# A hybrid attention, recurrence and latent-attention layer: sums of squares moved to VectorE, projection weights asked for earlier, and compression accumulators in other PSUM banks

## The chip, the cores and the metric

The kernel runs on one core of one Trainium2 chip. The metric is the device time of one execution in microseconds (us), given as the median of several runs. Five engines work side by side: TensorE (PE, with its weight loads as PEld), VectorE (DVE), ScalarE (ACT), GpSimd (POOL) and SyncE (SP, which only issues transfers here). Each takes its instructions in its own order and waits on semaphores for the others.

## The reference

One layer over 512 frames of 1024 channels (cut to what matters here):

```
h = rmsnorm(x, g_mix);  P = h @ w_in           # 7072 columns, split into parts
A: q, k, v 512 each     -> chunked banded softmax attention, 8 heads
B: q, f, i, g 512 each  -> HGRN2 gated recurrence, 8 heads
C: c_q 256, c_kv 128, k_rope 32 -> latent attention:
     q  = rmsnorm(c_q)  @ w_uq;  kv = rmsnorm(c_kv) @ w_ukv;  rotary on the rope parts
G: 3 x 1024 gate logits
x += (sum_n sigmoid(G_n) * (y_n @ w_branch[n])) @ w_out
x += relu(rmsnorm(x) @ w_ff1)^2 @ w_ff2;   out = rmsnorm(x)
```

All inputs and the output are float32.

## The kernel before

Activations are held transposed: channels on the 128 partitions, the 512 frames along the free dimension. Each float32 operand of a large product is split into a rounded high part and a low part (hi = the value cast to fp32r, lo = value - hi), and a product is three TensorE instructions, hi*hi, hi*lo and lo*hi (`mm3` at L225 to L228; `mm3_u` at L320 to L325 is the same with a stop after each). The mixing norm's gain is folded into x (`xgh`, `xgl`), and its row factor `rstd` is applied to the results afterwards, so that products can start before the norm is known.

**The order of work.** TensorE's instructions are issued in exactly the order of the program text. On all other engines and queues a planner lists the instructions ahead of time by its own estimate of when each is ready, with program order as priority; on the chip each engine then follows its list in order. Buffers of a tag (`bufs=3` and so on) are handed out by the planner as they come free, and whoever writes a reused buffer waits for its last reader.

**The opening stage (L340 to L430).** For each of the 8 channel blocks k, SP loads a block of x (`xt`) and half a block of the compression weights (`wc`, into one of two buffers `wr`). ScalarE makes `xgh` (L402), VectorE makes `xgl` (L403), `split` (L211 to L213) makes `wh` by ScalarE and `wl` by VectorE, and TensorE adds 12 products into four PSUM accumulators `pc` (c_q in two, c_kv, and the rotary key with its swapped copy). Two blocks k share one buffer `wh` and one `wl`; each of these tags has 3 buffers. ScalarE squares x (L419), and GpSimd adds the squares into `ss` (L421). At k = 2 the rotary angles are computed (`rotary`). The accumulators `pc0` to `pc2` take all three banks of the tag `acc`, `pc3` the one bank of `up`; the tags `sc` and `tp` have two banks each. After the loop the four accumulators are copied out to `c` (L427, L429).

**The queue of projections.** `project` (L432) and `project_nat` (L447) append units to a queue: 8 for the q and k of A (`aqk`, 24 products each, accumulated in an `acc` bank named `pj`), 2 for its v (`avn`), later those of B and the gates. `fill(n)` puts the next n products of the queue into TensorE's order wherever the text says so; the numbers stand in `TUNE`. Weights come through three steps: `load` asks for a 512 KB block on the POOL queue into a buffer of tag `wr` or `wh`, at most 2 ahead; `convert` lets ScalarE write its negated rounded copy into `wl` (L279), and a second, accumulating transfer of the same block on the POOL queue (L280) adds the weights to it, which leaves the low part. `get` takes the oldest converted block. `taken[0] % 5` chooses the tag:

```
tag, bufs = (("wr", 2), ("wh", 3))[taken[0] % 5 > 1]
```

**The norms (L480 to L510).** The squares of the three compressed blocks are made, `fill(s0 = 6)` puts in 6 products, and then three products with a matrix of ones sum over the channels: `pkv` (c_kv), `pst` (`ss`, the norm of x) and `pq` (c_q). VectorE and ScalarE turn these into `rk`, `rstd` and `rq` and scale the compressed blocks, and `fill(s1 = 30)` follows in TensorE's order.

**After that.** `csplit` splits the compressed blocks (`cnh`, `cnl`), `cweights` (L622) loads and splits small weight blocks, its low part by GpSimd, four products `pv` make C's v (banks `up`, `tp`, `sc`, `tp`), four steps prepare the first pair of heads, and the attention of C runs over 8 heads x 4 blocks of queries (`attention`, L568) with `fill` between its steps (`ca`, `cb`, `cd`). Up to the tail of that loop the fills take 281 of the 288 products in the queue; the rest goes into the tail. B's and the gates' units are appended only after it.

Of the kernel before, what the change touches and what calls it, by code (L numbers as in the profile page):

```python
# [32 lines left out]
PACE = 12  # L33

TUNE = dict(
    s0=6, s1=30, c0=3, c1=9, c2=18, ca=[5, 3, 3, 1, 3, 3, 3, 5], cb=[1, 0, 3, 5, 3, 1, 4, 4], cd=6, a0=9,
    aa=[7, 0, 6, 4], ab=[4, 2, 7, 5], ad=0, h0=60, ha=[7, 6, 5, 4, 5, 6, 2, 9, 3, 8, 5],
    hb=[8, 8, 5, 7, 6, 6, 5, 2, 20, 5, 4], n0=9,
)
# [101 lines left out]
def _body(ctx, tc, ap, dbgo):  # L141
# [8 lines left out]
    def f(t):  # L150
        return t.bitcast(F32)
# [12 lines left out]
    def acc(n="acc"):  # L164
        return ps.tile([P, S], F32, tag="acc", name=n, bufs=3)

    def pup(n="up"):
        return ps.tile([P, S], F32, tag="up", name=n, bufs=1)
# [4 lines left out]
    def ptp(n="tp"):  # L173
        return ps.tile([P, S], F32, tag="tp", name=n)
# [36 lines left out]
    def split(hi, lo, src):  # L211
        A.copy(hi, src)
        V.tensor_tensor(lo, src, f(hi), ALU.subtract)  # L213
# [11 lines left out]
    def mm3(out, wh, wl, xh, xl, start, stop, **kw):  # L225
        T.matmul(out, wh, xh, start=start, stop=False, **kw)  # L226
        T.matmul(out, wh, xl, start=False, stop=False, **kw)  # L227
        T.matmul(out, wl, xh, start=False, stop=stop, **kw)  # L228
# [34 lines left out]
    def load():  # L263

        while loads and len(raw) < 2:
            src = loads.pop(0)
            tag, bufs = (("wr", 2), ("wh", 3))[taken[0] % 5 > 1]
            taken[0] += 1
            hi = ws.tile([P, 1024], F32R, tag=tag, name="wh", bufs=bufs)
            G.dma_start(hi, src)  # L270
            raw.append((hi, src))
# [63 lines left out]
    with ExitStack() as st_ctx:  # L335
# [6 lines left out]
            T.matmul(warm[:, :P], ones, ones, start=True, stop=True)  # L342

        xt, wc = [], []
        pc = [acc(f"pc{i}") for i in range(3)] + [pup("pc3")]
        for k in range(NK):
            t = st.tile([P, S], F32, tag="xt", name="xt", bufs=8)
            nc.sync.dma_start(t, ap['xT'][k * P:(k + 1) * P, :])
# [12 lines left out]
        def rotary():  # L361

            def ct(n):
                return st.tile([P, 64], F32, tag="rp", name=n, bufs=6)
            pi = st.tile([P, 64], I32, name="rpi")
            G.dma_start(pi, bass.AP(tensor=ap['pos'].tensor, offset=0, ap=[[0, 16], [64, 8], [1, 64]]))
            ang = ct("ang")
            V.tensor_copy(ang, pi)
            V.tensor_scalar(ang, ang, freq, None, ALU.mult)
            n_ = ct("n_")  # L370
            V.tensor_scalar(n_, ang, 1.0 / (2 * np.pi), 12582912.0, ALU.mult, ALU.add)
            V.tensor_scalar(n_, n_, -12582912.0, None, ALU.add)
            rest = 2 * np.pi
            for i in range(5):
                part = float(np.float32(rest))
                if i < 4:
                    e = int(np.floor(np.log2(rest))) - 7
                    part = float(np.floor(rest / 2.0 ** e) * 2.0 ** e)
                rest -= part
                V.scalar_tensor_tensor(ang, n_, -part, ang, ALU.mult, ALU.add)  # L380
            V.tensor_scalar(ang, ang, -3.1415925, 3.1415925, ALU.max, ALU.min)
            sn = ct("sn")
            A.activation(sn, ang, AF.Sin)
            V.scalar_tensor_tensor(ang, ang, -1.0, ang, ALU.mult, ALU.max)
            cs = ct("cs")
            last_sin = A.activation(cs, ang, AF.Sin, bias=halfpi, scale=-1.0)
            tables("natural_log_exp_and_others", last_sin)
            return (("dcos", cs, cosT, 0, 4), ("dsin", sn, sinT, 2, 6))
# [5 lines left out]
                for i in range(first, first + n):  # L394
                    nc.sync.dma_start(dst[16 * i:16 * i + 16, :], d)

        make_identity(nc, ident)
        ss = st.tile([P, S], F32, name="ss")
        for k in range(NK):
            xh = act.tile([P, S], F32R, tag="act", name="xgh")  # L400
            xl = act.tile([P, S], F32R, tag="act", name="xgl")
            A.activation(xh, xt[k], AF.Copy, scale=g_mix[:, k:k + 1])  # L402
            V.scalar_tensor_tensor(xl, xt[k], g_mix[:, k:k + 1], f(xh), ALU.mult, ALU.subtract)  # L403
            xg.append((xh, xl))
            j = k % 2
            if j == 0:
                wh = ws.tile([P, 1024], F32R, tag="wh", name="wh")
                wl = ws.tile([P, 1024], F32R, tag="wl", name="wl")
            c = slice(j * 448, (j + 1) * 448)
            split(wh[:, c], wl[:, c], wc[k][:, c])  # L410
            for i in range(4):
                m = P if i < 3 else 64
                c = slice(j * 448 + i * P, j * 448 + i * P + m)
                mm3(pc[i][:m], wh[:, c], wl[:, c], xh, xl, k == 0, k == NK - 1)
            if k == 2:
                rotation = rotary()
            for j in (() if k == 0 else (k - 1,) if k < NK - 1 else (k - 1, k)):
                sq = ss if j == 0 else st.tile([P, S], F32, tag="sq", name="sq", bufs=2)
                A.activation(sq, xt[j], AF.Square)  # L419
                if j:  # L420
                    G.tensor_tensor(ss, ss, sq, ALU.add)  # L421
        crw = []
        for i in range(4):
            t = fqt(f"c{i}")
            m = P if i < 3 else 64
            if i % 2:
                V.tensor_copy(t[:m], pc[i][:m])  # L427
            else:
                A.copy(t[:m], pc[i][:m])  # L429
            crw.append(t)  # L430

        def project(src, n, name, out, then=None):  # L432
            def run():
                i = len(out)
                pz = acc("pj")
                yield from gemm_u(pz, get(), xg, NK)
                t = fqt(name)
                V.tensor_tensor(t, pz, rstd, ALU.mult)
                out.append(t)
                if then:  # L440
                    then(i, t)
                yield 1
            for i in range(n):
                last = add([src[i]], run)
            return last

        def project_nat(src, name, pool, out, halves=(0, 1)):  # L447

# [21 lines left out]
                last = add([src[half, kk] for kk in range(2)], half_run(half))  # L470
            return last

        aqk, avn, bz, bvn, bq, cums, late = [], [], [], [], [], [], {}
        project(ap['w_aqk'], 8, "aqk", aqk)
        a_done = project_nat(ap['w_av'], "avn", nap, avn)
        convert()
        convert()
        spread(rotation)

# [115 lines left out]
    with ExitStack() as at_ctx:  # L595
# [8 lines left out]
        with ExitStack() as c_ctx:  # L604
# [14 lines left out]
            ckv = [csplit(crw[2])]  # L619
            cqn = [csplit(t) for t in crw[:2]]  # L620

            def cweights(src, n):  # L622
                r = cp.tile([P, 640], F32, tag="cwr", name="cwr", bufs=1)
                nc.sync.dma_start(r[:, :n], src)
                hi = cp.tile([P, 640], F32R, tag="cwh", name="cwh", bufs=1)
                lo = cp.tile([P, 640], F32R, tag="cwl", name="cwl", bufs=1)
                A.copy(hi[:, :n], r[:, :n])
                G.tensor_tensor(lo[:, :n], r[:, :n], f(hi[:, :n]), ALU.subtract)
                return hi, lo


            wvh, wvl = cweights(ap['w_uv'], 512)
            v2 = []
            for s in range(NST):
                pv = (pup, ptp, psc, ptp)[s]("pv")
# [772 lines left out]
```

## Time and profile before

| | us |
|---|---|
| median of 3 runs | 954.14 |
| lowest and highest | 952.27 to 956.85 |
| the profiled execution's own time | 951.3 |
| its span in the trace | 949.5 |
| mean granted TensorE clock | 0.984 of full speed |

| engine | busy us | share of the span |
|---|---|---|
| PE | 907.1 | 96% |
| DVE | 657.1 | 69% |
| ACT | 557.5 | 59% |
| POOL | 201.4 | 21% |

The profiled execution's time is the span and 1.8 us around it. Times in the views are counted from the start of the span. The opening stage and the norms lie in its first 51 us, and the attention of C ends at about 164 us. A matmul's duration in a row is longer than its share of TensorE, since consecutive ones overlap; what counts is the distance from one start to the next.

### The profile page before, as it was taken

Reading aid. Unit: us, or ns where it says so; the run is one execution under the profiler, and the core shown is the slowest. Engines: PE = TensorE matmul, PEld = TensorE weight load, DVE = VectorE, ACT = ScalarE, POOL = GpSimd, SP = SyncE. Lnnn points to the kernel's source line nnn. Section 1 sums busy time; section 2 is a strip of 40 time slices with the busy share of each in tenths; the row PEclk is TensorE's granted clock in tenths of the full one; section 3 lists DMA queues with packets and bytes.
Section 4 is the critical chain, followed back from the end, with each engine's and each line's share of the span. In section 5 each row is a group of like instructions: output and inputs, shape, how many; then the busy total and the mean of one; then the engine's idle time right before and its main releaser. Section 6 shows DMA issues by size and latency. Waiting matters only on the chain.

```text
span 949.5 us, 13636 instructions
## 1 busy us (share of the span) xinstructions
PE 907.1 (96%) x5070; PEld 784.4 (83%) x5070; DVE 657.1 (69%) x1212; ACT 557.5 (59%) x983; POOL 201.4 (21%) x264
## 2 busy tenths in 40 slices
PE   8889999998998899999999999999999999999993
PEld 6578898987877788888888888889989988998992
DVE  6488888787878869788472454455456745885686
ACT  7556778787776656757552444555365346435663
POOL 4422101111154424333122122001101100110002
PEclk9899999999999999999999999999999999999996
DMA  6865445666666475758689784238835862893522
GB/s 200 212 132 120 91 93 115 140 123 125 139 128 144 97 157 111 155 115 195 137 203 207 165 236 140 89 92 196 227 108 133 209 190 89 182 240 111 132 47 89
DMA packets 42947, 138.08 MB, mean 145 GB/s; under 512 B 5056, under 2 KB 9296, under 8 KB 42880
## 3 DMA queue, kind: packets, MB, share of 16 engines
q0 software_dynamic: 23104, 83.95, 43.8%
q1 hardware_dynamic: 19776, 53.26, 16.8%
q8 instruction: 40, 0.66, 0.3%
q14 instruction: 27, 0.22, 0.1%
HBM read 135.03 MB, written 2.16 MB: 144 GB/s over the span
## 4 chain that ended last, share of the span: by engine, by line
PE 72%; DVE 15%; issue 4%; DMA 4%; ACT 3%; POOL 1%; SPq 0%; DVEq 0%; POOLq 0%; ACTq 0%
PE p L227 6%; PE p L228 6%; PE p L226 6%; PE pj L325 3%; PE pj L321 3%; PE pj L323 3%; PE pg L321 3%; PE pg L325 3%; PE pg L323 3%; PE sa L228 2%; PE sa L227 2%; PE sa L226 2%; PE sc L522 2%; DMA bias<-in_rel 2%; PE po L227 2%
## 5 line engine op out<-in xcount | busy, mean ns | idle before, releaser
L221 ACT CAST wh<-wr 128x1024 fp32r<-128x1024 f32 x64 | 67.2, 1050 | 111.0 <-PE p L227 24.8
L222 DVE TENSOR_TENSOR wl<-wr,wh 128x1024 fp32r<-128x1024 f32 x64 | 78.3, 1223 | 75.9 <-ACT wh L221 67.5
L226 PE MATMUL p<-x2h,wh 128*128 128x512 f32 x256 | 100.0, 391 | 0.0
L227 PE MATMUL p<-x2l,wh 128*128 128x512 f32 x256 | 99.6, 389 | 0.0
L228 PE MATMUL p<-x2h,wl 128*128 128x512 f32 x256 | 99.6, 389 | 0.0
L279 ACT ACTIVATE wl<-wh 128x1024 fp32r<-128x1024 f32 x64 | 67.7, 1057 | 48.4 <-PE pg L325 26.9
L321 PE MATMUL pg<-xgh,wh 128*128 128x512 f32 x192 | 76.7, 400 | 0.0
L325 PE MATMUL pg<-xgh,wl 128*128 128x512 f32 x192 | 76.6, 399 | 0.0
L323 PE MATMUL pg<-xgl,wh 128*128 128x512 f32 x192 | 76.3, 398 | 0.0
L321 PE MATMUL pj<-xgh,wh 128*128 128x512 f32 x160 | 65.0, 406 | 2.4 <-ACT c L429 2.4
L323 PE MATMUL pj<-xgl,wh 128*128 128x512 f32 x160 | 65.7, 410 | 0.0
L325 PE MATMUL pj<-xgh,wl 128*128 128x512 f32 x160 | 64.3, 402 | 0.8 <-DMA wl<-in_w_aqk 0.8
L1256 POOL DMA_DIRECT2D cw<-in_w_ff x16 | 13.7, 858 | 219.2 <-DVE wl L1236 216.4
L226 PEld LDWEIGHTS p<-x2h,wh 128*128 128x128 f32 x256 | 48.1, 188 | 10.1 <-issue 0.2
L227 PEld LDWEIGHTS p<-x2l,wh 128*128 128x128 f32 x256 | 48.1, 188 | 10.1 <-issue 0.2
L228 PEld LDWEIGHTS p<-x2h,wl 128*128 128x128 f32 x256 | 48.1, 188 | 10.0
L227 PE MATMUL sa<-rl,wh 128*128 128x256 f32 x192 | 54.3, 283 | 0.0
L228 PE MATMUL sa<-rh,wl 128*128 128x256 f32 x192 | 54.3, 283 | 0.0
L226 PE MATMUL sa<-rh,wh 128*128 128x256 f32 x192 | 54.3, 283 | 0.0
L1236 DVE TENSOR_TENSOR wl<-cw,wh 128x1024 fp32r<-128x1024 f32 x24 | 29.3, 1223 | 29.9 <-ACT wh L1235 29.9
L1235 ACT CAST wh<-cw 128x1024 fp32r<-128x1024 f32 x24 | 25.2, 1050 | 35.0 <-PE sc L227 11.1
L321 PEld LDWEIGHTS pg<-xgh,wh 128*128 128x128 f32 x192 | 36.9, 192 | 7.8 <-DVE tg L884 0.4
(406 smaller groups left out, 2807.7 us busy)
## 6 DMA issues: line engine op xcount, KB each, us to landing
wr<-in_w_ff SPq DMA_DIRECT2D x56, 512.0 KB, 3.5
wh<-in_w_g POOLq DMA_DIRECT2D x24, 512.0 KB, 3.9
wl<-in_w_g POOLq DMA_DIRECT2D x24, 512.0 KB, 6.1
cw<-in_w_ff POOLq DMA_DIRECT2D x24, 512.0 KB, 5.6
wh<-in_w_br POOLq DMA_DIRECT2D x12, 512.0 KB, 3.8
wl<-in_w_br POOLq DMA_DIRECT2D x12, 512.0 KB, 6.1
wh<-in_w_aqk POOLq DMA_DIRECT2D x8, 512.0 KB, 4.4
wl<-in_w_aqk POOLq DMA_DIRECT2D x8, 512.0 KB, 6.4
```

The costliest lines, as they stand in the source:

```text
L221: A.copy(hi[:, :n], r[:, :n])
L222: (eng or G).tensor_tensor(lo[:, :n], r[:, :n], f(hi[:, :n]), ALU.subtract)
L226: T.matmul(out, wh, xh, start=start, stop=False, **kw)
L227: T.matmul(out, wh, xl, start=False, stop=False, **kw)
L228: T.matmul(out, wl, xh, start=False, stop=stop, **kw)
L279: A.activation(lo, f(hi), AF.Copy, scale=-1.0)
L321: T.matmul(out, wh, xh, start=start, stop=False, **kw)
L323: T.matmul(out, wh, xl, start=False, stop=False, **kw)
L325: T.matmul(out, wl, xh, start=False, stop=stop, **kw)
L522: T.matmul(sc[:, :n], l[:, t * P:(t + 1) * P], r[:, :n], start=i == 0, stop=i == len(scores) - 1)
L1235: A.copy(hi, r)
L1236: V.tensor_tensor(lo, r, f(hi), ALU.subtract)
```

## The change

- **Squares:** the additions into `ss` go from GpSimd to VectorE (7 of them). The squares are made one step later (blocks 0 and 1 at k = 2).
- **First step:** at k = 0 the weights are split before `xgh` and `xgl` are made; at the other k the order stays.
- **Weights of the projections:** `aqk` is put into the queue inside the loop, after the products of k = 4, with a `load()` there, and the first `convert()` comes at k = 6. One `convert()` is left behind the loop.
- **Buffers of the loads:** the first three of every five go into `wh`, the other two into `wr` (before: the first two into `wr`).
- **Banks:** `pc0` in `acc`, `pc1` and `pc2` in `tp`, `pc3` in `up` as before.
- **`s1`:** 36 products behind the norms' sums, before 30.
- **`cweights` for C's v:** its low part is made by VectorE.

```diff
-    s0=6, s1=30, c0=3, c1=9, c2=18, ...
+    s0=6, s1=36, c0=3, c1=9, c2=18, ...
...
-            tag, bufs = (("wr", 2), ("wh", 3))[taken[0] % 5 > 1]
+            tag, bufs = (("wr", 2), ("wh", 3))[taken[0] % 5 < 3]
...
-        pc = [acc(f"pc{i}") for i in range(3)] + [pup("pc3")]
+        pc = [acc("pc0"), ptp("pc1"), ptp("pc2"), pup("pc3")]
...
         for k in range(NK):
...
+            if k == 0:
+                split(wh[:, c], wl[:, c], wc[k][:, c])
             A.activation(xh, xt[k], AF.Copy, scale=g_mix[:, k:k + 1])
             V.scalar_tensor_tensor(xl, xt[k], g_mix[:, k:k + 1], f(xh), ALU.mult, ALU.subtract)
             xg.append((xh, xl))
...
-            split(wh[:, c], wl[:, c], wc[k][:, c])
+            if k:
+                split(wh[:, c], wl[:, c], wc[k][:, c])
             for i in range(4):
...
             if k == 2:
                 rotation = rotary()
-            for j in (() if k == 0 else (k - 1,) if k < NK - 1 else (k - 1, k)):
+            if k == 4:
+                project(ap['w_aqk'], 8, "aqk", aqk)
+                load()
+            if k == 6:
+                convert()
+            for j in (() if k < 2 else (k - 2, k - 1) if k == 2 else (k - 1,) if k < NK - 1 else (k - 1, k)):
                 sq = ss if j == 0 else st.tile([P, S], F32, tag="sq", name="sq", bufs=2)
                 A.activation(sq, xt[j], AF.Square)
                 if j:
-                    G.tensor_tensor(ss, ss, sq, ALU.add)
+                    V.tensor_tensor(ss, ss, sq, ALU.add)
...
-        project(ap['w_aqk'], 8, "aqk", aqk)
         a_done = project_nat(ap['w_av'], "avn", nap, avn)
         convert()
-        convert()
...
-            def cweights(src, n):
+            def cweights(src, n, eng=None):
...
-                G.tensor_tensor(lo[:, :n], r[:, :n], f(hi[:, :n]), ALU.subtract)
+                (eng or G).tensor_tensor(lo[:, :n], r[:, :n], f(hi[:, :n]), ALU.subtract)
...
-            wvh, wvl = cweights(ap['w_uv'], 512)
+            wvh, wvl = cweights(ap['w_uv'], 512, V)
```

`project` itself moves up in the text unchanged, so that the loop can call it.

## Rows read from the trace of the kernel before

**Rows 1.** Busy time by stretch: us, length, PE PEld DVE ACT POOL, PEclk, DMA, GB/s.

```profile
7.19:29.95 22.76, 22.58 (x96) 16.58 (x96) 18.47 (x27) 16.13 (x27) 13.40 (x15) 1.00 0.72 214
29.95:39.88 9.93, 6.73 (x13) 3.43 (x13) 2.40 (x4) 4.64 (x7) 3.68 (x5) 0.66 1.04 239
39.88:50.70 10.82, 8.15 (x35) 5.91 (x33) 8.45 (x15) 6.67 (x11) 1.43 (x2) 1.00 0.61 135
50.70:157.50 106.80, 106.56 (x624) 92.95 (x624) 93.66 (x240) 76.86 (x169) 20.78 (x24) 1.00 0.53 111
157.50:164.50 7.00, 5.47 (x41) 4.67 (x40) 4.84 (x10) 6.07 (x13) 1.11 (x2) 1.00 0.44 105
```

**Rows 2.** TensorE's waits, first 60 us: us in total, times, longest.

```profile
PE pj L321 <- ACT c L429: 2.4, 1, 2.4
...
PE pv L228 <- DVE cnl L213: 1.6, 1, 1.6
...
PE pv L226 <- ACT cnh L212: 1.1, 1, 1.1
PE pj L325 <- DMA wl<-in_w_aqk: 0.8, 1, 0.8
```

**Rows 3.** Timeline of TensorE, 24 to 60 us: start, us, instruction, idle before it.

```profile
24.05 0.39 PE L228 MATMUL pc<-xgh,wl 128*64 128x512 f32 x1
...
29.56 0.39 PE L228 MATMUL pc<-xgh,wl 128*64 128x512 f32 x1
32.30 0.66 PE L321 MATMUL pj<-xgh,wh 128*128 128x512 f32 x1 [2.36 <-ACT c L429]
...
36.12 1.91 PE L492 MATMUL pkv<-csq,ones 128*128 128x512 f32 x2
37.82 1.76 PE L493 MATMUL pst<-ss,ones 128*128 128x512 f32 x2
...
50.70 0.50 PE L228 MATMUL pv<-cwh,cnl 128*128 128x512 f32 x1 [1.61 <-DVE cnl L213]
```

**Rows 4.** Timeline of VectorE, 24 to 60 us.

```profile
34.47 0.86 DVE L489 TENSOR_TENSOR csq<-csq 128x512 f32<-128x512 f32 x1 [3.25 <-ACT csq L488]
39.62 0.69 DVE L498 TENSOR_SCALAR vx<-pst 128x512 f32<-128x512 f32 x1 [4.28 <-PE pst L493]
```

**Rows 5.** Timeline of ScalarE, 24 to 60 us.

```profile
30.72 1.06 ACT L279 ACTIVATE wl<-wh 128x1024 fp32r<-128x1024 f32 x1 [3.10 <-DVE c L427]
31.68 1.06 ACT L429 COPY c<-pc 128x512 f32<-128x512 f32 x2
...
47.68 0.62 ACT L212 CAST cnh<-c 128x512 fp32r<-128x512 f32 x1
```

**Rows 6.** Timeline of GpSimd, 20 to 60 us.

```profile
28.54 0.94 POOL L280 DMA_DIRECT2D wl<-in_w_aqk  x1
```

**Rows 7.** Timeline of TensorE, 290 to 300 us.

```profile
297.05 0.36 PE L226 MATMUL sl<-qbh,kxh 128*128 128x256 f32 x1 [2.65 <-ACT d L988]
```

**Rows 8.** Timeline of all engines, first 20 us.

```profile
6.59 0.55 ACT L212 CAST wh<-wr 128x448 fp32r<-128x448 f32 x1
...
7.19 0.50 PE L226 MATMUL pc<-xgh,wh 128*128 128x512 f32 x1 [1.24 <-ACT wh L212]
...
7.42 0.62 DVE L213 TENSOR_TENSOR wl<-wr,wh 128x448 fp32r<-128x448 f32 x1
...
8.10 0.50 PE L228 MATMUL pc<-xgh,wl 128*128 128x512 f32 x1 [0.17 <-DVE wl L213]
```

**Rows 9.** Groups of instructions, first 30 us: busy, mean ns, idle before.

```profile
L421 POOL TENSOR_TENSOR ss<-ss,sq 128x512 f32<-128x512 f32 x7 | 10.2, 1453 | 11.8 <-DMA dcos<-cs 6.1 <-ACT sq L419 5.5
...
L403 DVE SCALAR_TENSOR_TENSOR xgl<-xt,cst,xgh 128x512 fp32r<-128x512 f32 x8 | 7.8, 980 | 2.2 <-ACT xgh L402 2.2
L213 DVE TENSOR_TENSOR wl<-wr,wh 128x448 fp32r<-128x448 f32 x8 | 7.3, 912 | 0.0
```

**Rows 10.** DMA issues of the first 60 us: KB each, median us to landing.

```profile
wl<-in_w_aqk POOLq DMA_DIRECT2D x5, 512.0 KB, 6.8
```

More of the change, by code (lines that the diff above doesn't have):

```diff
@@ L35 @@
 TUNE = dict(
-    s0=6, s1=30, c0=3, c1=9, c2=18, ca=[5, 3, 3, 1, 3, 3, 3, 5], cb=[1, 0, 3, 5, 3, 1, 4, 4], cd=6, a0=9,
+    s0=6, s1=36, c0=3, c1=9, c2=18, ca=[5, 3, 3, 1, 3, 3, 3, 5], cb=[1, 0, 3, 5, 3, 1, 4, 4], cd=6, a0=9,
     aa=[7, 0, 6, 4], ab=[4, 2, 7, 5], ad=0, h0=60, ha=[7, 6, 5, 4, 5, 6, 2, 9, 3, 8, 5],
@@ L395, in spread @@
                     nc.sync.dma_start(dst[16 * i:16 * i + 16, :], d)
[L397 to L409, printed above, removed]
-            split(wh[:, c], wl[:, c], wc[k][:, c])
[L411 to L416, printed above, removed]
-            for j in (() if k == 0 else (k - 1,) if k < NK - 1 else (k - 1, k)):
-                sq = ss if j == 0 else st.tile([P, S], F32, tag="sq", name="sq", bufs=2)
-                A.activation(sq, xt[j], AF.Square)
-                if j:
-                    G.tensor_tensor(ss, ss, sq, ALU.add)
[L422 to L430, printed above, removed]
         def project(src, n, name, out, then=None):
@@ L445, in project @@
             return last
+        make_identity(nc, ident)
+        aqk, avn, bz, bvn, bq, cums, late = [], [], [], [], [], [], {}
+        ss = st.tile([P, S], F32, name="ss")
+        for k in range(NK):
+            xh = act.tile([P, S], F32R, tag="act", name="xgh")
+            xl = act.tile([P, S], F32R, tag="act", name="xgl")
+            j = k % 2
+            if j == 0:
+                wh = ws.tile([P, 1024], F32R, tag="wh", name="wh")
+                wl = ws.tile([P, 1024], F32R, tag="wl", name="wl")
+            c = slice(j * 448, (j + 1) * 448)
+            if k == 0:
+                split(wh[:, c], wl[:, c], wc[k][:, c])
+            A.activation(xh, xt[k], AF.Copy, scale=g_mix[:, k:k + 1])
+            V.scalar_tensor_tensor(xl, xt[k], g_mix[:, k:k + 1], f(xh), ALU.mult, ALU.subtract)
+            xg.append((xh, xl))
+            if k:
+                split(wh[:, c], wl[:, c], wc[k][:, c])
+            for i in range(4):
+                m = P if i < 3 else 64
+                c = slice(j * 448 + i * P, j * 448 + i * P + m)
+                mm3(pc[i][:m], wh[:, c], wl[:, c], xh, xl, k == 0, k == NK - 1)
+            if k == 2:
+                rotation = rotary()
+            if k == 4:
[4 more added lines that the diff above has]
+            for j in (() if k < 2 else (k - 2, k - 1) if k == 2 else (k - 1,) if k < NK - 1 else (k - 1, k)):
+                sq = ss if j == 0 else st.tile([P, S], F32, tag="sq", name="sq", bufs=2)
+                A.activation(sq, xt[j], AF.Square)
+                if j:
+                    V.tensor_tensor(ss, ss, sq, ALU.add)
+        crw = []
+        for i in range(4):
+            t = fqt(f"c{i}")
+            m = P if i < 3 else 64
+            if i % 2:
+                V.tensor_copy(t[:m], pc[i][:m])
+            else:
+                A.copy(t[:m], pc[i][:m])
+            crw.append(t)
         def project_nat(src, name, pool, out, halves=(0, 1)):
@@ L471, in project_nat @@
             return last
-        aqk, avn, bz, bvn, bq, cums, late = [], [], [], [], [], [], {}
-        project(ap['w_aqk'], 8, "aqk", aqk)
         a_done = project_nat(ap['w_av'], "avn", nap, avn)
-        convert()
         convert()
```

## The prediction

> **What bounds the kernel now.** I read the page first: TensorE is busy for 96% of the span, so only time in which it waits or runs slowly can be won. The table by stretch then shows where that lies near the change [rows 1]. From 7.19 to 29.95 us (the compression products) and from 50.70 to 157.5 us TensorE is busy all but 0.4 us in all, at a granted clock of 1.00. Between them lie 20.75 us with 14.9 us of busy time, and in the first half the granted clock is 0.66. The list of TensorE's waits names what is missing [rows 2]: 2.4 us until ScalarE has copied out an accumulator, 0.8 us for the low weights of the first projection, and 2.7 us for the scaled c_kv, high part and low part.
>
> The timeline of TensorE gives the order [rows 3]. The compression products end at T0 = 29.56 + 0.39 = 29.95 us. The first projection product starts at 32.30, the sum `pkv` at 36.12, `pst` at 37.82, and the reader should see that a sum takes 1.70 us from start to start here. VectorE starts on the result of `pst` (`vx`) at 39.62 [rows 4]. The product that waits for the low part of c_kv starts at 50.70 [rows 3].
>
> ScalarE's timeline says why the first wait is so long [rows 5]. Its copy of the accumulators (L429) starts only at 31.68, since the negated copy for the second weight block (L279), which stands ahead of it in the list, had waited until 30.72. The row names VectorE's copy as releaser, but that would not hold up this instruction; what it reads is the block being loaded. GpSimd asks for the first low weights at 28.54 [rows 6].
>
> The clock: after 2.36 us of idle time TensorE ran at the lower level, 1.2 GHz. At 297.05 us a wait of 2.65 us did not lower it [rows 7]. So a short gap may cost clock or not, and I treat that as a chance and not as a rule.
>
> **The change, part by part.** *First step.* ScalarE's cast of the first weights starts at 6.59, the first product follows it by 0.60 us, and the third waits for VectorE until 8.10 [rows 8]. With the split first, ScalarE casts before the first `xgh` and squares nothing before the weights. The third product is then held by `xgl` rather than by `wl`; it can come some 0.7 us earlier: the 0.60 us from the cast to the first product and the 0.17 us of waiting for `wl` leave the way. The planner may keep its old order: bounds 0 and 0.7. I take -0.7, because the text's order is the planner's priority.
>
> *Additions on VectorE.* On GpSimd they took 1453 ns each. While they ran, VectorE's own work was stretched: its groups have means of 980 and 912 ns, while one of the second form that ran before them took 0.62 [rows 8, 9]; if the first form takes 0.7 alone, that is some 4.5 us lost over 8 of each. On VectorE an addition of the same shape took 0.86 us [rows 4], so 7 cost at most 6.0 us. VectorE is busy 18.47 of 22.76 us in the stretch, some 4.5 us of it that stretching [rows 1]: about 14 + 6.0 = 20 fits. On the path I take 0 (bounds 0 and 4.2, seven times 0.6, if each addition stands ahead of a part that TensorE needs). The Trainium skill, page "SBUF — State Buffer", section "SBUF: two separate sides", has the read and write port pair of VectorE and GpSimd as an exclusive lock that is held for the whole instruction when VectorE has two SBUF inputs. By that rule the stretching goes entirely and VectorE gains more than it takes on; if instead nothing of it goes, the 18.47 us become 24.5 and TensorE loses about 1.7 us. The stretched rows agree with the rule.
>
> *Weight buffers at k = 6.* This part costs. The three `wh` buffers hold blocks 0-1, 2-3 and 4-5 when the new `load()` at k = 4 asks for two more. Those two take the buffers of blocks 0-1 and 2-3 as they come free. Blocks 6-7, which found a free buffer before, must then wait until TensorE has read the last of block 5 (its last product starts at 24.05 [rows 3]; the one ahead of it is the last to read `wh`). Then comes the cast, 0.60 us to the first product and 1.51 us to the third [rows 8]. TensorE has 0.23 us of its own left, and two products of 0.23 between the first and the third, so it stands for about 0.5 + 0.45 = 1.0 us. Bounds: 0 if the planner gives out the buffers otherwise, 2.0 if a negated copy of 1.06 us [rows 5] stands just ahead on ScalarE. Sum so far: T0 moves by -0.7 + 1.0 = +0.3, to 30.25 us.
>
> *Banks and early loads.* `pj` finds an `acc` bank free, so the 2.36 us wait goes if the weights are there. The first block can be asked for at about 13 us, when blocks 0 and 1 are done (24 products of 0.23 from 7.6), instead of behind GpSimd's additions. Its negated copy comes at k = 6, at 20 to 24 us, so the low weights land 6.8 us [rows 10] and about 1 us of copying later, at 28 to 31.5 us; needed at 30.25 + 0.46 = 30.7. I take them as in time; if not, see the first rival. The second block is loaded by then too, so that ScalarE's list no longer holds up the copies. Without the gap I take the clock as full. From T0 to `vx` it was 39.62 - 29.95 = 9.67 us. It becomes 6 products of 0.23 us (24 products in 29.56 - 24.05 = 5.51), 1.38 us; two sums at half of the 1.70 and 1.60 us seen at the low clock, 1.65; and 0.20 to VectorE as before: 3.23 us. That is **-6.4 us**. It can be no more than this by this way, and nothing if the weights come late.
>
> *Six more products.* From `vx` to the product at 50.70 it is 11.08 us, a chain of VectorE and ScalarE that stays [rows 3, 4]. `pq` (0.8 us, begun 0.2 us before `vx`) and 36 products of 0.23 us, 8.3 in all, end at `vx` + 8.9; the high part of c_kv is there at 47.68 + 0.62 = `vx` + 8.7 [rows 5]. So the six end inside the 2.7 us of waiting and cost nothing there (1.4 us if the chain were shorter). They gain nothing either: they are missing in the tail of C's attention, where TensorE is busy only 5.47 of 7.00 us and ScalarE 6.07 [rows 1], so that their going frees no time I can count on (bounds 0 and -1.4).
>
> *The rest.* The low part of C's v weights on VectorE is 0.7 us in a stretch in which it is busy 2.40 of 9.93 us [rows 1]; were it full, the norms would come 0.7 us later. The later pattern of buffers is the same cycle of five, shifted, so each load still waits for the one five before it: 0. From 50.70 us on TensorE does the same work in the same order, and what is won there stays won to the end.
>
> **Sum.** -0.7 + 1.0 - 6.4 = -6.1 us. The profiled execution goes from 951.3 to 945.2 us. The median lies 2.84 us above the profiled one, so it goes from 954.14 to about **948.0 us**, 0.64% less. Its own range: all bounds in favour (no stop at k = 6, 1.4 us in the tail) give -8.5 and 945.6; the upper bound at k = 6 and a negated copy of 1.06 us falling into the norm's chain give -4.0 and 950.1.
>
> **Rivals.**
>
> *The low weights come late.* They land at 34.2 us as before. For it: transfers through 30 us keep the DMA engines busy at 0.72 already [rows 1]. Against it: the request need no longer queue behind additions. Then TensorE starts two products, waits, and goes on from 34.24 as before: 0, 954.1 us. The same page of the Trainium skill, in its box on VectorE blocking transfers asked for by GpSimd, says descriptors can't be written while VectorE runs an instruction in a two-port mode. That would make this case likelier, but no row here shows such a delay.
>
> *VectorE becomes the bound* of the opening stage: 4.2 us are lost there, -1.9 in all, 952.2 us. Against it stands the arithmetic above.
>
> *The tail gives it back.* Without the six products TensorE idles more before 164.5 us, the clock falls, and some 7.6 us (as from 32.30 to 39.9) run at half speed: +3.8, so -2.3 and 951.8 us. For it: ScalarE bounds that stretch; against it: the gaps there now, 1.5 us together, cost no clock [rows 1].
>
> *Slower: the third load blocks the second low weights.* In program order the third `load` stands ahead of the second accumulating transfer on GpSimd's queue, and its `wh` buffer may come free only when the first unit is done: T0 + 1.4 (6 products) + 2.5 (three sums) + 18 x 0.23 = 38.3 us. Then the low weights of unit 2 land near 45.7 [rows 10], 7 us after TensorE wants them. 18 products are left at half speed, 0.43 us each, about two of them started: the norm's product comes near 53 us instead of 50.70, 956.5 us, and over 958.9 if the clock stays low until 58 us. It decides once those weights land after about 43.4 us. Against it: before, too, the planner put a transfer ahead of one that stood earlier in the text when its buffer was free first.
>
> **Chances.** About 0.5% (4.8 us) can be told from no change. Forecast 0.58, of which 0.53 beyond 949.4 us and 0.05 within; late weights 0.15 (0.11 within, 0.04 slower with a late second block as well); VectorE 0.06 and the tail 0.10, both within; blocked queue 0.11 (0.03 within, 0.08 slower). Together: faster 0.53, same 0.35, slower 0.12. The range 945.2 to 954.8 holds the forecast's own range and the three rivals that end near no change.
>
> **What the profile will show.** Right: the third product near 7.4 us; a stop of about 1 us at the first product of k = 6; the first `pj` within 0.5 us of the last `pc`; a granted clock of 1.00 from 30 to 40 us; `vx` near 33.5 and the product after the low part of c_kv near 44.6 us; from there all shifted by 6 us. Wrong: a wait of `pj` on a transfer, a low clock behind it or near 160 us, VectorE named in waits of `pc`, or a GpSimd request waiting for `pj` before the second accumulating transfer.

## The result, and the profile after

The changed kernel takes 958.41 us (median of 14 runs, 953.23 to 962.0) against 954.09 us (14 runs, 951.35 to 956.85): a ratio of 1.004 with a 95% interval of 1.0026 to 1.0054. It is slower by 0.4%, where 0.64% faster was forecast; 958.4 lies above the range. The profiled execution took 958.5 us, its span 956.6.

The table by stretch of the changed kernel, with its borders at the steps of [rows 1], the last stretch longer because C's attention ends later (us, length, busy time of PE, PEld, DVE, ACT and POOL, granted clock, DMA share, GB/s):

```profile
7.19:33.79 26.60, 24.60 (x97) 17.69 (x97) 17.22 (x36) 17.98 (x31) 3.98 (x6) 0.94 0.75 226
33.79:39.14 5.35, 3.41 (x11) 1.83 (x11) 1.38 (x3) 1.63 (x3) 0.55 (x1) 1.00 1.02 247
157.50:170.00 12.50, 9.48 (x50) 7.90 (x50) 9.09 (x17) 9.54 (x19) 1.40 (x2) 0.86 0.43 88
```

The compression products end at T0 = 33.79 us, 3.84 later than before. From there to `vx` it is 5.35 us instead of 9.67, at full clock. So 4.3 us of the hoped-for gain came; but the later T0 took 3.8 of them back, and the product after the low part of c_kv starts at 50.21 us, only 0.5 earlier. At the end of C's attention the clock, 1.00 before, is 0.86 on average.

TensorE's timeline between (start, us, line; the idle time before and its releaser in brackets):

```profile
24.08 0.39 PE L228 MATMUL pc<-xgh,wl 128*64 128x512 f32 x1
24.89 0.49 PE L226 MATMUL pc<-xgh,wh 128*128 128x512 f32 x1 [0.43 <-ACT wh L212]
...
26.90 0.50 PE L228 MATMUL pc<-xgh,wl 128*128 128x512 f32 x1 [1.27 <-DVE wl L213]
...
28.01 0.63 PE L226 MATMUL pc<-xgh,wh 128*128 128x512 f32 x1
28.43 0.63 PE L227 MATMUL pc<-xgl,wh 128*128 128x512 f32 x1
...
30.99 0.51 PE L227 MATMUL pc<-xgl,wh 128*128 128x512 f32 x1
31.34 0.39 PE L228 MATMUL pc<-xgh,wl 128*128 128x512 f32 x1
...
33.62 0.39 PE L321 MATMUL pj<-xgh,wh 128*128 128x512 f32 x1
...
36.19 0.50 PE L325 MATMUL pj<-xgh,wl 128*128 128x512 f32 x1 [1.94 <-DMA wl<-in_w_aqk]
...
50.21 0.50 PE L228 MATMUL pv<-cwh,cnl 128*128 128x512 f32 x1 [1.59 <-DVE cnl L213]
```

At k = 6 TensorE stops twice, 1.70 us in all. From 28.01 to 30.99 the products come 0.43 us apart instead of 0.23. That is the lower clock level; it lasts for seven products and costs, with the change of level, some 1.6 us. The stops with their restarts make the other 2.2 us of the 3.8 that the last 24 products lost. Then the first low weights are missing for 1.94 us.

The other engines say why. ScalarE, VectorE and GpSimd in the same stretch:

```profile
24.28 1.03 ACT L212 CAST wh<-wr 128x448 fp32r<-128x448 f32 x2 [1.45 <-PE pc L227]
25.22 2.00 ACT L279 ACTIVATE wl<-wh 128x1024 fp32r<-128x1024 f32 x2
```

```profile
25.71 0.48 DVE L617 TENSOR_SCALAR sinT<-sinT,cst 32x512 f32<-32x512 f32 x1 [2.16 <-DMA sinT<-dsin]
26.22 1.16 DVE L213 TENSOR_TENSOR wl<-wr,wh 128x448 fp32r<-128x448 f32 x2
...
39.14 0.69 DVE L504 TENSOR_SCALAR vx<-pst 128x512 f32<-128x512 f32 x1 [2.99 <-PE pst L499]
```

```profile
13.53 0.57 POOL L270 DMA_DIRECT2D wh<-in_w_aqk  x1 [9.66 <-DVE ss L445]
17.82 0.53 POOL L270 DMA_DIRECT2D wh<-in_w_aqk  x1 [3.73 <-DVE wl L213]
19.03 0.53 POOL L270 DMA_DIRECT2D wh<-in_w_aqk  x1 [0.68 <-PE pc L228]
27.68 0.53 POOL L270 DMA_DIRECT2D wh<-in_w_aqk  x1 [8.11 <-DVE wl L213]
28.20 1.84 POOL L280 DMA_DIRECT2D wl<-in_w_aqk  x2
```

ScalarE's cast for blocks 6 and 7 waits for TensorE's last read of block 5, since the early loads took the buffers that were free before. The two negated copies stand behind the cast. VectorE's `wl` for block 6, ready to run at about 24.8, stands behind the multiplication of the sine table, which waits for its transfer until 25.71. On GpSimd's queue the fourth load waits for that very split until 27.68 (by the order of tags it goes into the `wr` buffer that the split reads), and both accumulating transfers stand behind the load. So the first low weights, asked for at 28.54 before [rows 6], are asked for at 28.20: queueing, loading and converting inside the loop won 0.3 us.

The end of C's attention: ScalarE before, then after, and then TensorE's waits, before and after:

```profile
159.76 0.84 ACT L465 ACTIVATE avn<-pv,rstdn 128x256 f32<-128x256 f32 x2
160.50 0.48 ACT L212 CAST pTh<-tp 128x384 fp32r<-128x384 f32 x1
160.86 0.86 ACT L465 ACTIVATE avn<-pv,rstdn 128x256 f32<-128x256 f32 x2
162.09 0.59 ACT L212 CAST pTh<-tp 128x512 fp32r<-128x512 f32 x1 [0.37 <-PE tp L547]
162.57 1.06 ACT L279 ACTIVATE wl<-wh 128x1024 fp32r<-128x1024 f32 x1
```

```profile
160.95 1.57 ACT L474 ACTIVATE avn<-pv,rstdn 128x256 f32<-128x256 f32 x4
162.40 0.50 ACT L212 CAST pTh<-tp 128x384 fp32r<-128x384 f32 x1
162.76 1.09 ACT L279 ACTIVATE wl<-wh 128x1024 fp32r<-128x1024 f32 x1
163.72 0.61 ACT L212 CAST pTh<-tp 128x512 fp32r<-128x512 f32 x1
```

```profile
PE tp L547 <- DVE pTl L213: 0.6, 1, 0.6
PE av L563 <- ACT pTh L212: 0.7, 1, 0.7
```

```profile
PE tp L553 <- DVE pTl L213: 1.6, 1, 1.6
PE av L569 <- ACT pTh L212: 1.4, 1, 1.4
```

ScalarE's list has changed places: all four `avn` copies now stand ahead of the 384-wide cast of `pTh`, and the negated copy ahead of the 512-wide one. TensorE's waits there grow from 1.5 to 3.0 us (0.2 us of the 1.5 is a third, short wait). With the lower clock behind them, the way from the product after the low part of c_kv to the first product behind the tail takes 116.9 us instead of 113.9. One more loss stands in this trace, far from the change:

```profile
493.98 0.50 PE L325 MATMUL pg<-xgh,wl 128*128 128x512 f32 x1 [2.91 <-DMA wl<-in_w_g]
```

With the low clock behind it, that costs 4.8 us in this execution: the gate products run 1.96 us later than before ahead of the wait and 6.76 us later behind it. The profile after is 7.1 us longer than the one before, while the medians differ by 4.3. The wait is at least in part chance (last section).

### The profile page after: what moved, and what is told of

It is laid out like the page before. It is cut to its first block, busy times and chain, and to the rows that moved or that the text cites. A ratio compares the mean times of both kernels' runs of the same rounds, so it can differ in the third digit from the quotient of the medians.

```text
span 956.6 us, 13640 instructions
## 1 busy us (share of the span) xinstructions
PE 909.7 (95%) x5070; PEld 787.1 (82%) x5070; DVE 654.1 (68%) x1220; ACT 557.9 (58%) x983; POOL 190.4 (20%) x256
## 4 chain that ended last, share of the span: by engine, by line
PE 69%; DVE 15%; issue 6%; DMA 5%; ACT 4%; POOL 1%; DVEq 0%; SPq 0%; POOLq 0%; ACTq 0%
PE p L226 6%; PE p L227 6%; PE p L228 6%; PE pg L325 3%; PE pg L321 3%; PE pg L323 3%; PE pj L321 3%; PE pj L325 2%; PE pj L323 2%; PE sa L228 2%; PE sa L227 2%; PE sa L226 2%; DMA bias<-in_rel 2%; PE po L227 2%; PE sc L528 2%
## 5 line engine op out<-in xcount | busy, mean ns | idle before, releaser
L279 ACT ACTIVATE wl<-wh 128x1024 fp32r<-128x1024 f32 x64 | 67.6, 1058 | 49.0 <-PE pg L325 30.7
L325 PEld LDWEIGHTS pg<-xgh,wl 128*128 128x128 f32 x192 | 37.2, 194 | 10.7 <-DMA wl<-in_w_g 3.3
```

The lines of the kernel that those rows point to most:

```text
L279: A.activation(lo, f(hi), AF.Copy, scale=-1.0)
```

## The experiments

The theory after the first reading: the early asks with their buffer order lose what the rest wins, and the six products cost something in C's attention. The rivals: the additions on VectorE are the price, or the banks, or all comes from the tail. Each kernel was compared with the kernel before on the same chip. A ratio below 1 is faster than before, and where its 95% interval (in brackets) holds 1, no difference is shown. The medians of before were 953.13 (first four), 953.55 (next four) and 954.38 us (last four).

**30 products again**, all else as changed.

```diff
-    s0=6, s1=36, ...
+    s0=6, s1=30, ...
```

> The changed kernel with 30 products behind the norms' sums, as before. Theory: the six more products are missing in the tail of C's attention, where TensorE then waits 3.0 us and its clock falls, and they move the ends of the units to worse places in the loop; together about 3 us of the 7 by which the profiled executions differ. Then this kernel is 2 to 3 us faster than the changed one (955.5 to 956.5), TensorE's waits between 161 and 166 us come to 1.5 us and not 3.0, and the granted clock there is 1.00. Rival: the tail is ScalarE's and VectorE's in any case, and the time is that of the changed kernel within 1 us.

Measured: 954.74 us, ratio 1.0009 (0.9991 to 1.0027). TensorE's waits in the tail are 0.63 and 0.67 us as before; the stops at k = 6 stay (0.43 and 1.82 us), and so does the wait for low weights (2.50 us). The six products are some 3 us of the loss, not all.

**The six products alone**, in the kernel before (`s1=36`).

> The kernel before with 36 products behind the norms' sums and nothing else of the change. Theory of the six products: 2 to 3 us slower than before (956 to 957), with waits of 3 us in the tail of C's attention. Rival, and the prediction as it stood: they end inside the waits for the scaled c_kv and cost nothing, 954 within 1 us.

Measured: 957.62 us, ratio 1.0048 (1.003 to 1.0066). By itself this edit costs 0.5%. TensorE, the last compression product and the product after the low part of c_kv:

```profile
31.20 0.39 PE L228 MATMUL pc<-xgh,wl 128*64 128x512 f32 x1
...
52.33 0.50 PE L228 MATMUL pv<-cwh,cnl 128*128 128x512 f32 x1 [1.34 <-DVE cnl L213]
```

The second row is 1.6 us later than before, but so is the first: this execution began late (third product at 9.00 us), ahead of anything that the edit touches. From T0 on it takes 20.74 us, before 20.75, so the six products cost nothing by the norms. C's attention and its tail take 116.4 us instead of 113.9, with the waits of the changed kernel in the tail (1.63 and 1.38 us).

**A buffer of its own for blocks 6 and 7**, in the changed kernel: the early loads stay, the slot wait goes.

```diff
-                wh = ws.tile([P, 1024], F32R, tag="wh", name="wh")
+                wh = (st if k == 6 else ws).tile([P, 1024], F32R, tag="wh", name="wh")
```

> The changed kernel, but the high weights of blocks 6 and 7 get a buffer of their own, so that they needn't wait for that of blocks 4 and 5. Theory of the buffers: the wait of 0.4 + 1.3 us at k = 6, the low clock behind it, the negated copies and GpSimd's transfers that came late with it, all go back to this one buffer; the compression products end near 29.8 us and not 33.8, the product after the low part of c_kv starts near 44.5 us and not 50.2, and the time is 5 to 6 us below that of the changed kernel, near 953. Rival: the low weights are late for the transfers' sake; then the products end earlier, but the first projection waits longer, and the time stays within 1.5 us of 958.4.

Measured: 953.24 us, ratio 1.0000 (0.9979 to 1.0021), 0.4% less than the changed kernel. GpSimd's queue, TensorE and VectorE there:

```profile
22.02 0.89 POOL L280 DMA_DIRECT2D wl<-in_w_aqk  x1 [2.39 <-ACT wl L279]
```

```profile
PE pq L500 <- DVE csq L495: 2.4, 1, 2.4
```

```profile
33.56 0.49 DVE L617 TENSOR_SCALAR sinT<-sinT,cst 64x512 f32<-64x512 f32 x1 [4.15 <-DMA sinT<-dsin]
34.07 0.68 DVE L451 COPY c<-pc 64x512 f32<-64x512 f32 x1
34.79 0.69 DVE L495 TENSOR_TENSOR csq<-csq 128x512 f32<-128x512 f32 x1
35.40 0.68 DVE L504 TENSOR_SCALAR vx<-pst 128x512 f32<-128x512 f32 x1
```

No stop at k = 6, the low weights asked for at 22.02 and in time, `pj` right behind the last `pc`, `pst` at 32.14: so far the opening is as forecast. Then comes another wait: VectorE stands at the sine table for 4.15 us, with the copy of the fourth accumulator and `csq` behind it, and `vx` comes at 35.40 us instead of 33.5. The product after the low part of c_kv starts at 47.25 us, where 44.5 was expected, so the kernel gains 0.4%, some 4 us, on the changed one and not the expected 5 to 6 us.

**Late asks**, with the changed squares, banks, first step and 36 products: queue, load, first conversion and tag order as before.

```diff
-            tag, bufs = (("wr", 2), ("wh", 3))[taken[0] % 5 < 3]
+            tag, bufs = (("wr", 2), ("wh", 3))[taken[0] % 5 > 1]
...
-            if k == 4:
-                project(ap['w_aqk'], 8, "aqk", aqk)
-                load()
-            if k == 6:
-                convert()
...
+        project(ap['w_aqk'], 8, "aqk", aqk)
         a_done = project_nat(ap['w_av'], "avn", nap, avn)
         convert()
+        convert()
```

> The changed kernel without the early asks: queue, first load and both conversions behind the loop, and the old order of buffers; the additions on VectorE, the banks, the first step and the 36 products stay. Theory of the buffers: no wait at k = 6, the products end near 29.9 us; the low weights land some 1 to 2 us sooner than before, since GpSimd has no additions; the product after the low part of c_kv starts near 48 to 49 us, and the time is 955 to 956 with what the six products cost. It also asks for the wait of 2.9 us at 494 us: if the new order of the buffers makes it, it is gone here and stands in the two kernels above that keep that order; if it is chance, it stands in any.

Measured: 952.22 us, ratio 0.9995 (0.9975 to 1.0016). Without any early ask `pj` waits only 0.37 us for low weights, and the product after the low part of c_kv starts at 45.30 us, 5.4 earlier than before and some 3 earlier than expected. "Late" is the place in the text: in the planner's lists the first low weights are asked for at 23.78 us all the same, 4.4 us ahead of the changed kernel. C's attention and its tail (waits of 1.65 and 1.38 us), with the lower clock behind them, give 3.7 of the 5.4 us back.

**Late asks and 30 products.**

> The kernel with late asks and 30 products behind the norms' sums instead of 36. Theory of the six products: the 5.4 us won by 50 us stay, since the loop of C's attention and its tail get the fill that they had before; waits of 1.5 us and not 3.0 in the tail, about 948 us, 4 to 5 us below before. Rival: the six filled the norms' wait, TensorE stops there for 1.4 us more and its clock falls, and the time is that with 36, near 952.

Measured: 947.68 us, ratio 0.9945 (0.992 to 0.9969). The same product at 44.96 us, the tail's waits 0.63 and 0.67.

**Late asks, 36 products, and six fewer (`c2=12`) in the last fill ahead of C's attention**: the 36 stay by the norms, but the queue stands where it stood before when the attention begins.

> The kernel with late asks, 36 products behind the norms' sums, and 6 fewer behind the preparation of C's first heads (c2 = 12), so that the loop of C's attention meets the queue at the old place. Theory: what costs is that the queue runs out six products sooner and the results of A's v come sooner to ScalarE, in the loop and in its tail; with the place restored the time is that of 30 products, about 948, if TensorE has no new wait before the loop. Rival: 36 products behind the sums are themselves too many there; then this kernel stays near 952.

Measured: 948.45 us, ratio 0.9949 (0.993 to 0.9967). TensorE's waits in the tail:

```profile
PE av L566 <- ACT pTh L212: 0.7, 1, 0.7
PE tp L550 <- DVE pTl L213: 0.6, 1, 0.6
```

So 36 products by the norms cost nothing there. What costs is that the queue is six products ahead when the attention begins: in the four profiles with six ahead (the changed kernel, the six products alone, own buffer, late asks) the way through C's attention and its tail takes 116.4 to 116.9 us, in the seven with the queue at its old place and the full clock at the start of this stretch 113.8 to 113.9 (in three more of the runs below the lower clock reaches into it).

**Only the additions on VectorE**, in the kernel before: one line.

```diff
-                    G.tensor_tensor(ss, ss, sq, ALU.add)
+                    V.tensor_tensor(ss, ss, sq, ALU.add)
```

> The kernel before with only the additions of the squares on VectorE. Theory: GpSimd's queue asks for the low weights at about 27 us and not 28.5, VectorE's parts are no longer stretched; the accumulators still fill all three banks, so the wait of 2.4 us for their copies stays unless the second block lands sooner; the product after the low part of c_kv starts 1 to 3 us earlier, 951 to 953. Rival: VectorE becomes the bound of the opening and the products end later than 29.95 us.

Measured: 948.57 us, ratio 0.9956 (0.9934 to 0.9978). Nearly all the gain that any version has is in this line (the best ratios of other versions are 0.9945 to 0.9952), and it is more than the 1 to 3 us that were expected. GpSimd's queue, TensorE, and the table by stretch with the borders of [rows 1]:

```profile
17.66 0.56 POOL L270 DMA_DIRECT2D wh<-in_w_aqk  x1 [13.79 <-DVE wl L213]
...
23.37 0.90 POOL L280 DMA_DIRECT2D wl<-in_w_aqk  x1 [0.63 <-ACT wl L279]
```

```profile
31.10 0.50 PE L325 MATMUL pj<-xgh,wl 128*128 128x512 f32 x1 [0.84 <-DMA wl<-in_w_aqk]
...
45.12 0.50 PE L228 MATMUL pv<-cwh,cnl 128*128 128x512 f32 x1 [1.61 <-DVE cnl L213]
```

```profile
7.19:29.95 22.76, 22.34 (x97) 16.61 (x97) 15.82 (x33) 17.36 (x29) 3.73 (x6) 1.00 0.88 244
29.95:39.88 9.93, 9.09 (x35) 6.22 (x34) 5.32 (x9) 6.48 (x11) 3.42 (x5) 1.00 0.94 222
```

Without the additions in front the first load is asked for at 17.66 us and the first low weights at 23.37, where before it was 28.54 [rows 6]. The negated copies, the copies of the accumulators and the sums follow earlier, and the low clock from 30 to 40 us is gone although `pc` still takes the `acc` banks. The compression products themselves end at 29.79 us, only 0.16 earlier; nearly all of the 5.6 us that are won at 45.12 lies behind them. VectorE takes on the additions and is less busy than before (15.82 us against 18.47 in the first stretch).

**Only the banks**, in the kernel before.

```diff
-        pc = [acc(f"pc{i}") for i in range(3)] + [pup("pc3")]
+        pc = [acc("pc0"), ptp("pc1"), ptp("pc2"), pup("pc3")]
```

> The kernel before with only the compression accumulators in other banks. Theory: two products of the first projection start at once at 30 us, the third waits for the low weights until 34.2 us as before, since GpSimd's queue is the same; nothing is won, 954 within 1 us. Rival: the free banks alone keep the clock up, and 3 us are won.

Measured: 954.28 us, ratio 1.0004 (0.9982 to 1.0026). `pj` no longer waits for its bank and waits 4.32 us for its low weights instead, until 35.73 us.

**Own buffer and 30 products.**

> The changed kernel with the weights still asked for early, blocks 6 and 7 in a buffer of their own, and 30 products by the norms again. Theory (the stop at k = 6 and the six products are the two prices, and they add): 953.2 us of the own buffer alone less the 4.5 us that the six products cost with late asks, so about 948.7 us, with the tail's waits at 0.6 and 0.7 us. Rival (the early asks have another price behind the first products, VectorE's list standing at the sine table): TensorE's pq again near 35.5 us behind VectorE's csq, and the time one to two us over the 947.7 of late asks, which would be 949 to 950. Rival (the two prices are one, so that taking the first away also takes the second): 953 as with the own buffer alone.

Measured: 949.97 us, ratio 0.9952 (0.9928 to 0.9976). The two prices add, as the theory said: 0.5% less than with 36. `pq` waits 0.9 us behind `csq`, so the rival's wait is there too; what it costs can't be told, since the ratio lies within the interval of late asks with 30 products and this execution ran its first products at the lower clock (T0 at 31.54 us).

**The sine table's multiplication written behind C's v sums**, in the run before.

```diff
-            for a in (slice(32, 64), slice(64, 128)):
-                V.tensor_scalar(sinT[a], sinT[a], sgn[a], None, ALU.mult)
...
+            for a in (slice(32, 64), slice(64, 128)):
+                V.tensor_scalar(sinT[a], sinT[a], sgn[a], None, ALU.mult)
             t1, t2 = ctmp("kr1"), ctmp("kr2")
```

> The run before (own buffer, 30 products) with the multiplication of the sine table by its signs written behind C's four v sums instead of ahead of them. Theory (it stood ahead of VectorE's copy of the fourth accumulator and of csq, and waited 4.2 us for the table): vx comes near 33.5 us instead of 35.4, no low clock at 37 to 39.5 us, and 1 to 2.5 us less than the run before. Rival (the norm's chain is held by ScalarE or TensorE in the same place): vx moves by less than 0.5 us and the time stays.

Measured: 949.81 us, ratio 0.9948 (0.9927 to 0.9969). This edit didn't do what its name says: the planner left the multiplication where it was in VectorE's list (33.08 us here, still ahead of the copy and of `csq`). It is a repetition of the run before, and the price of the sine table stays untested.

**The same edit on late asks with 30 products.**

> The best run so far (late asks, 30 products, 947.7 us) with the sine table's signs multiplied behind C's v sums. Theory (VectorE's 2.7 us at the sine table, to 32.0 us, hold csq and vx by about 0.5 to 1 us there): 947 us, vx near 33.2 instead of 33.9. Rival: no change, 947.7.

Measured: 951.69 us (945.6 to 954.68), ratio 0.9963 (0.9937 to 0.9988). Again the lists kept their order, so this repeats the 947.68 us run: the medians of two such series differed by 4 us, the ratios by 0.2%. Smaller differences between series are not read here.

**Only one block asked for early**, in the changed kernel with 30 products and no added buffer: `load` and `convert` take a limit, 1 at k = 4 and k = 6.

```diff
-    def load():
+    def load(most=2):
-        while loads and len(raw) < 2:
+        while loads and len(raw) < most:
...
-                load()
+                load(1)
             if k == 6:
-                convert()
+                convert(1)
```

> The changed kernel with 30 products, and only one block of the first projection asked for at k = 4 instead of two; no buffer added. Theory (it is the second early load that takes the buffer of blocks 6 and 7 and puts a load ahead of the low weights on GpSimd's queue): no stop at k = 6, the first low weights asked for near 22 us and there in time, no wait of pj over 0.5 us, and some 947 to 950 us, against 954.7 with two blocks. Rival (any early ask costs, by its cast and copy on ScalarE among the compression's): the stop stays, 953 to 955 us.

Measured: 952.01 us, ratio 0.9977 (0.9955 to 1.0000). That is less gain than expected (947 to 950 us). The limit holds only for the first `load` of each call: the `load` at the end of `convert` still asks for two, and GpSimd's queue has two more requests from 24.73 us on. The stop at k = 6 is gone and the first low weights are in time, but the second block, which is one of these two, lands so late that its negated copy holds up ScalarE's copy of an accumulator:

```profile
32.72 1.06 ACT L279 ACTIVATE wl<-wh 128x1024 fp32r<-128x1024 f32 x1 [3.89 <-DMA wh<-in_w_aqk]
33.69 0.57 ACT L453 COPY c<-pc 128x512 f32<-128x512 f32 x1
```

```profile
PE pkv L498 <- ACT csq L494: 3.3, 1, 3.3
```

That is the wait of the kernel before [rows 5] in a new place: `vx` comes at 38.49 us.

**The account.** In per cent of the time before: the additions on VectorE -0.4 (alone) to -0.5 (late asks with 30 products, which has the banks, the first step, the later squares and VectorE's low part of C's v weights as well); the early asks with their buffers +0.45 (1.0040 against 0.9995 with late asks) to +0.55 (1.0009 against the mean of 0.9945 and 0.9963); the six products +0.5 in the kernel before, +0.3 in the changed one (1.0040 against 1.0009), +0.4 with late asks and +0.5 with the own buffer. Together that is about +0.3 to +0.6, an estimate, since each part was measured beside other parts; measured +0.4.

## Why the prediction was wrong, step by step

The forecast was -6.1 us; the medians differ by +4.3, the profiled executions by +7.1. Against the forecast the profiled execution lost 0.7 us in the first step, 2.8 in the weight buffers at k = 6, 2.1 in the early loads, some 3.4 through the six products, and 4.8 at the wait near 494 us, which is no step of the prediction and at least in part chance.

*First step:* -0.7 was taken, 0 was right. ScalarE's list kept the old order, `xgh`, square, cast (5.14, 5.76, 6.29 us), and the third product came at 8.12 us as before. The bound of 0 named it. VectorE's first work also stood behind the transfer of the positions until 6.28 us, which the prediction left out.

*Additions on VectorE:* it was right that VectorE has room; wrong was where the worth of it was booked. It was put at 0 on the path, and the -6.4 us were given to banks and early loads. The banks alone bring nothing, and the early loads cost; the additions alone bring 0.4%. The prediction saw the link ("instead of behind GpSimd's additions") but took the early ask as what undoes it. VectorE's groups in the changed kernel (mean in ns last, against 980 and 912 in [rows 9]):

```profile
L426 DVE SCALAR_TENSOR_TENSOR xgl<-xt,cst,xgh 128x512 fp32r<-128x512 f32 x7 | 5.2, 746 | 0.0
L213 DVE TENSOR_TENSOR wl<-wr,wh 128x448 fp32r<-128x448 f32 x8 | 4.9, 619 | 0.0
L445 DVE TENSOR_TENSOR ss<-ss,sq 128x512 f32<-128x512 f32 x7 | 4.8, 686 | 1.5 <-ACT sq L443 1.4
```

The stretching went with GpSimd's additions. The Trainium skill, page "SBUF — State Buffer", section "SBUF: two separate sides", has a lock that a VectorE instruction with two SBUF inputs and a GpSimd instruction that reads SBUF can only hold one after the other; the trace agrees. An addition takes 0.69 us on VectorE and not the 0.86 of the sum: the row of 0.86 [rows 4] overlaps GpSimd's `cwl` (33.19 to 34.78 us), and the same instruction takes 0.69 in the changed kernel (35.45 us).

*Weight buffers at k = 6:* this is the step that failed first, and the next one failed through it. The mechanism was named and its place was right, but its price was mis-sized: +1.0 was taken, 2.0 was the bound, +3.84 at T0 came. Two things were not in the sum for T0: VectorE's `wl` behind the sine table (the second stop was 1.27 us, not 0.45) and the lower clock behind the two stops (some 1.6 us). A third, the negated copies that came late behind the cast, carried the stop into the next step.

*Banks and early loads:* -6.4 was taken, 9.67 - 5.35 = -4.3 came. The clock was full from 33.8 us on and the first `pj` followed at once. The low weights were forecast to land at 28 to 31.5 us; `pj` got them at 36.19. (By the prediction's own figures the later bound is 24 + 6.8 + 1 = 31.8, past the 30.7 at which they were needed.) The cause was not the 6.8 us of the transfer but the ask at 28.20, behind the slot wait and behind a load that waited at the head of GpSimd's queue. That is the first rival's wait, two us longer than priced there, by the fourth rival's mechanism: the blocked load struck the first two blocks, where the rival had only the second and a buffer that comes free 10 us later. Once the slot wait is taken away (own buffer) the low weights are in time and `pst` starts 2.1 us behind T0, as forecast; but `vx` still comes 5.35 us behind T0, now because of the sine table, which the prediction didn't have. Late asks with 30 products come nearest to the forecast's 3.23 us, with 3.87.

*Six more products:* this step failed too, and by as much: 0 was taken, +0.3 to +0.5% came. By the norms they are free, as said (late asks: 45.30 against 44.96 us; in the kernel before: 20.74 against 20.75 us from T0). They cost in C's attention, where the queue is six products further on, conversions and `avn` copies fall at other places, and ScalarE's list puts them ahead of what TensorE needs. The third rival (the tail) had the sign, the place and the clock. Its reason was not quite it: with six fewer products in the fill ahead of the attention the loss goes. That the lists' order is what costs was read from the tail; within the loop it was not followed.

*VectorE as the bound* did not come true in the opening's products; where VectorE did stop the work it stood at a transfer, not at additions. Of the prediction's signs of being wrong three came: the wait of `pj` on a transfer, a low clock near 160 us, and VectorE named in a wait of `pc` (26.90 us).

## What to carry to other kernels

Before an early ask is counted as a gain, follow who loses the buffer that it takes, and what stands behind the loser on each in-order queue: here one slot wait stopped TensorE, lowered its clock and delayed the very transfer that was to come early. Elementwise work on the engine that issues transfers is paid for in requests that stand behind it: moving seven additions off GpSimd was worth as much, within the intervals, as the best version of all edits together. Moving products between fills moves everything that is counted by the queue; check the other end of the queue before calling it free. And a place in the text is not a place in time where a planner makes the lists: late asks were listed early, and the sine table did not move.

## What the runs showed of the hardware

The lower clock followed two short waits (0.43 us ahead of 24.89 and 1.27 us ahead of 26.90) and a wait of 2.91 us at 493.98, but not the 1.94 us at 36.19 and not the 2.65 us of [rows 7]. At the same wait near 494 us it also followed 1.90 us (banks alone) and 2.51 us (late asks, sine table later), but not 2.14 us (own buffer, 30 products). In the tail of C's attention it followed all four pairs of waits of 1.62 to 1.65 and 1.38 to 1.40 us, and none of the ten pairs of 0.6 and 0.7 us. In the profile of late asks with the sine table later it followed the waits at C's v sums (1.07 and 1.61 us; products at the lower level from 48.38 to 53.92 us), which left it full in the kernel before (1.05 and 1.61). So the length of a wait alone did not decide it here.

Executions of one program already differ in their first microseconds. VectorE's cast of the positions waits for a small transfer that lets it start, over the 14 profiles, at 6.1 to 7.7 us, and the first `xgl` stands behind it. Late asks with 30 products and its repetition with the sine table have the same lists; the cast starts at 6.19 us in the first and here in the second:

```profile
7.65 0.20 DVE L368 CAST ang<-rpi 128x64 f32<-128x64 int32 x1 [2.08 <-DMA rpi<-in_pos]
```

There the third product came at 9.49 us instead of 8.17, the clock was low from 9.97 to 12.96 us, and T0 was 32.91 us instead of 30.01. In the same two profiles the wait for low gate weights near 494 us was 2.51 us and none. Over the 14 profiles it was between 0 and 2.9 us, also in kernels with the old buffer order (1.9 us with the banks alone, 0.6 with the six products alone, none in the kernel before); what sets it was not settled.
